# Sixteen gate panels of an encoder layer as four plain panels and six seven-product pairs, and a convolution that adds nine of its taps by transfers

## The chip, the cores and the metric

The kernel runs on one core of a Trainium2 chip. Times are device microseconds (us) of one execution of the whole program; a kernel's time is the median of its runs. The engines are called as in the profile: PE multiplies matrices, DVE is the vector engine, ACT the scalar engine, POOL the GpSimd engine, SP only issues transfers. Each engine works through its own queue in order. POOL's queue holds transfers too: one that waits for a semaphore holds back everything behind it.

## The reference

Two encoder layers on 528 positions (16 meta tokens and 512 tokens) by 2048 channels. What the change touches lies in the first:

```python
u = rmsnorm(h, norm_g)
proj = jnp.einsum("bld,de->ble", u, w_in)
z_a, xs, Bm, Cm, dt_f, dt_b, z_b, glu_v, glu_g = split_cols(proj, IN_E_SIZES)
y_a = ssd_mixer(xs, Bm, Cm, dt_f, dt_b, z_a, ...)
# conformer_conv: GLU, a 31-tap depthwise convolution, LayerNorm over channels, SiLU
y_b = conformer_conv(glu_v, glu_g, dw_w, dw_b, ln_g, ln_b) * jax.nn.silu(z_b)
return h + jnp.einsum("ble,ed->bld", jnp.concatenate([y_a, y_b], axis=-1), w_out)
```

The second layer (neighbourhood attention) and the final norm are not touched.

## The kernel before, in words

Activations lie with channels on the partitions: a tile is 128 channels by 528 positions, 16 tiles for 2048 channels. A **panel** is 128 output columns of a weight. `proj` multiplies one panel: both factors are split in a high and a low part (`wh`, `wl` of the weight, `rh`, `rl` of the input), three products are kept, and with 16 tiles of input and two halves of 264 positions that is 96 matmuls of 128x264. `fetch` makes the halves of a weight: a transfer to `raw`, a copy on ACT to `wh` (L256), a subtraction on DVE to `wl` (L259).

A **seven-product pair** (`sproj`) makes two panels at once by a scheme with seven block products in place of eight: 168 matmuls for 192. It needs sums of weight blocks (`block_ops`; a transfer with accumulation on POOL's queue, L169, and additions on DVE, L176), seven blocks per pair, sums of input tiles (`combos`, L803, eight of them, each with four half-tile additions and two splits on DVE; the tiles come in by transfers to a ring of slots `srt`), and merging additions (`merge`). The last of the sums is written over the split input itself (`fourth`, tiles `sr4`). A `phase` first makes four plain panels while the sums are formed, then six pairs.

The program runs in this order.

- **Scan and GLU stage**: the panels of the state-space scan, group by group, and between them the GLU panels. Each finished GLU tile `u` (buffer `up`) goes to `conv31` (L438): two taps on ACT as the start of `a0` and `a1`, 29 taps as multiply-and-add on DVE (L447), alternately into `a0` and `a1`, their sum (L449), a store to `cv_d`, and an addition to `accl`. A queue `bgc` holds the convolutions; `step` lets some taps run after every panel. The POOL multiplication `sg` (L656) stands before the multiplication into `u` (L659).
- **Second gate** (L743 to L758): 16 plain panels `z_b`, each evacuated by DVE (L746) with SiLU on ACT, all kept in SBUF. Remaining taps run there, then the LayerNorm `ln`: a column sum of `accl` on PE gives the mean, 16 tiles are loaded from `cv_d` into 16 buffers, the mean is subtracted (L722), squares are summed, the reciprocal root is made, and each tile is scaled (L737), gets SiLU, is multiplied by its gate (L739) and stored to `yb_d`.
- **Phases a, b, c** (L920): the output projection over `yz_d` (a), over `yb_d` (b), and the next layer's projections (c), each four panels and six pairs. The next phase's input is split during the last pair of the one before.

The order on each engine is not the order of the text: a scheduler orders the recorded instructions by its own estimate of when each is ready.

Of the kernel before, what the change touches and what calls it, by code (L numbers as in the profile page):

```python
# [12 lines left out]
F32 = mybir.dt.float32  # L13
# [4 lines left out]
P = 128  # L18
# [45 lines left out]
EARLY = 4  # L64
SRB, SRC = 5, 3
# [17 lines left out]
def hybrid_encoder(ctx: ExitStack, tc: tile.TileContext, hT, win, wdt, wout, oin, oout, par, con,  # L83
# [34 lines left out]
    yz_d = dr.tile([KT, P, L], F32, name="yz_d")  # L118
    cv_d = dr.tile([KT, P, L], F32, name="cv_d")
# [9 lines left out]
    gcut = [0, 1, 2, 3, 4, 6, 7, 8, 10]  # L129
# [6 lines left out]
    panels += [win[48 + m] for m in range(KT)]  # L136
    vqk = [oin[b + p] for p in range(KT) for b in (32, 0, 16)]
    for seq in ([wout[0, (m + 2 * NORM) % KT] for m in range(KT)], [wout[1, m] for m in range(KT)], vqk):
        panels += seq[:2 * NORM]
        panels += [(seq[2 * j], seq[2 * j + 1], 3 if j == NORM else int(2 * j + 2 == len(seq))) for j in range(NORM, len(seq) // 2)]  # L140
# [229 lines left out]

    gstack = ctx.enter_context(ExitStack())
    gp = gstack.enter_context(tc.tile_pool(name="gp", bufs=1))

    with ExitStack() as c0:
# [63 lines left out]
        def conv31(i, u):  # L438
            wv = lambda j: pr("dw", KC * i + j, KC * i + j + 1)
            a0 = gp.tile([P, L], F32, name="a0", tag="a0", bufs=1)  # L440
            a1 = gp.tile([P, L], F32, name="a1", tag="a1", bufs=1)
            nc.scalar.activation(a0, u[:, 15:15 + L], AF.Identity, bias=pr("db", i, i + 1), scale=wv(15))  # L442
            nc.scalar.activation(a1, u[:, 14:14 + L], AF.Identity, scale=wv(14))
            rest = [j for j in range(KC) if j not in (14, 15)]
            for q, j in enumerate(rest):
                a = (a0, a1)[q % 2]
                nc.vector.scalar_tensor_tensor(a, u[:, j:j + L], wv(j), a, op0=ALU.mult, op1=ALU.add)  # L447
                yield 620
            nc.vector.tensor_tensor(a0, a0, a1, op=ALU.add)  # L449
            nc.gpsimd.dma_start(cv_d[i], a0)  # L450
            yield 620
            if i == 0:
                nc.scalar.activation(accl, a0, AF.Copy)
            else:
                nc.vector.tensor_tensor(accl, accl, a0, op=ALU.add)
            yield 620
# [16 lines left out]
        sg0 = gp.tile([P, L], F32, name="sg", tag="sig", bufs=1)  # L473
# [173 lines left out]
        def step():  # L647
            pump(bgs, SB_)
            pump(bgc, CB_)

        def glu_tile(i):
            ps = proj(us, ls)
            sg = gp.tile([P, L], F32, name="sg", tag="sig", bufs=1)
# [4 lines left out]
            ps = proj(us, ls)  # L658
            u = gp.tile([P, L + KC - 1], F32, name="up", tag="up", bufs=3)  # L659
# [31 lines left out]
    srn = [0]  # L691

    def slot(name="srt"):
        i = srn[0] % (SRB + SRC) if len(sr) > 1 else 0
        srn[0] += 1
        return sr[i >= SRB].tile([P, L], F32, name=name, tag="srt")
# [6 lines left out]

    ready = {}

    with ExitStack() as c1:
        psb = c1.enter_context(pool(name="psc", bufs=1, space=bass.MemoryType.PSUM))
        zb = c1.enter_context(pool(name="zbp", bufs=14))
        big = c1.enter_context(pool(name="big", bufs=16))
        rp = c1.enter_context(pool(name="rp", bufs=1))  # L710
        mu = accl
        zbs = []
        xc = []
        acq = rp.tile([P, L], F32, name="acq")

        def ln():
            nc.vector.tensor_scalar_mul(h2(mu), colsum([accl], psb, "cs"), 1.0 / D)
            yield 600
            for i in range(KT):
                t = big.tile([P, L], F32, name="xc", tag="xc")  # L720
                nc.gpsimd.dma_start(t, cv_d[i])
                nc.vector.tensor_tensor(t, t, mu, op=ALU.subtract)  # L722
                xc.append(t)
                sq = tp.tile([P, L], F32, name="sq", tag="st", bufs=2)
                if i == 0:
                    nc.scalar.activation(acq, t, AF.Square)
                else:
                    nc.scalar.activation(sq, t, AF.Square)
                    nc.vector.tensor_tensor(acq, acq, sq, op=ALU.add)
                yield 1250  # L730
            rsl = mu
            rstd_row(acq, L, CH, psb, "cs", rsl)
            yield 1500
            for i in range(KT):
                while len(zbs) <= i:
                    yield 1000
                nc.vector.scalar_tensor_tensor(xc[i], xc[i], pr("lg", i, i + 1), rsl, op0=ALU.mult, op1=ALU.mult)  # L737
                nc.scalar.activation(xc[i], xc[i], AF.Silu, bias=pr("lb", i, i + 1))
                nc.vector.tensor_tensor(xc[i], xc[i], zbs[i], op=ALU.mult)  # L739
                nc.gpsimd.dma_start(yb_d[i], xc[i])  # L740
                yield 1250

        for m in range(KT):  # L743
            ps = proj(us, ls)
            t = zb.tile([P, L], F32, name="zb", tag="zb")
            nc.vector.tensor_tensor(h2(t), ps, rs0h, op=ALU.mult)  # L746
            nc.scalar.activation(t, t, AF.Silu)
            zbs.append(t)
            if bgc:
                pump(bgc, 7000)  # L750
# [848 lines left out]
```

## Time and profile before

| | us |
|---|---|
| median of 3 runs (lowest, highest) | 2637.94 (2636.39, 2638.48) |
| the profiled execution | 2635.41 |
| its span | 2633.6 |
| PE busy | 2599.0 (99%) |
| DVE busy | 2050.0 (78%) |
| ACT busy | 1417.3 (54%) |
| POOL busy | 363.2 (14%) |
| first and last evacuation of the second gate (L746) | 1109.2, 1289.3 |
| first and last scaling in phase a (L961) | 1307.0, 1462.2 |
| last sum of a convolution's two halves (L449) | 1183.1 |

All rows of the trace are of this one execution, 2.5 us under the median. Its span leaves 1.8 us outside. A duration in a row is that of one instruction alone; when DVE's instructions follow each other closely, the next one starts before the last has ended, so a queue's pace is read from the starts in a timeline and not from the durations.

### The profile page before, as it was taken

Reading aid. Unit: us, or ns where it says so; the run is one execution under the profiler, and the core shown is the slowest. Engines: PE = TensorE matmul, PEld = TensorE weight load, DVE = VectorE, ACT = ScalarE, POOL = GpSimd, SP = SyncE. Lnnn points to the kernel's source line nnn. Section 1 sums busy time; section 2 is a strip of 40 time slices with the busy share of each in tenths; the row PEclk is TensorE's granted clock in tenths of the full one; section 3 lists DMA queues with packets and bytes.
Section 4 is the critical chain, followed back from the end, with each engine's and each line's share of the span. In section 5 each row is a group of like instructions: output and inputs, shape, how many; then the busy total and the mean of one; then the engine's idle time right before and its main releaser. Section 6 shows DMA issues by size and latency. Waiting matters only on the chain.

```text
span 2633.6 us, 52655 instructions
## 1 busy us (share of the span) xinstructions
PE 2599.0 (99%) x21236; PEld 2485.8 (94%) x21236; DVE 2050.0 (78%) x3046; ACT 1417.3 (54%) x2636; POOL 363.2 (14%) x586
## 2 busy tenths in 40 slices
PE   8999999999999999999999999999999999999997
PEld 8999999999999999999999999999999987777797
DVE  6985967887686969997688888877777776666886
ACT  5366585666658566325554556633334355656543
POOL 0000000000000001100220312200000043443133
PEclk9999999999999999999999999999999999999999
DMA  4222223222222222533875877755555554443755
GB/s 173 98 76 93 81 77 97 81 94 74 92 85 76 88 90 92 177 108 112 266 234 166 296 217 229 239 159 157 157 156 148 151 144 134 135 131 117 232 171 166
DMA packets 147140, 373.40 MB, mean 142 GB/s; under 512 B 32704, under 2 KB 50784, under 8 KB 146896
## 3 DMA queue, kind: packets, MB, share of 16 engines
q1 hardware_dynamic: 121872, 290.09, 34.2%
q0 software_dynamic: 23008, 78.30, 11.2%
q8 instruction: 167, 2.74, 0.4%
q10 hardware_dynamic: 2016, 1.65, 0.2%
q14 instruction: 77, 0.63, 0.1%
HBM read 320.59 MB, written 49.38 MB: 140 GB/s over the span
## 4 chain that ended last, share of the span: by engine, by line
PE 88%; DVE 4%; ACT 4%; issue 2%; DMA 2%; POOL 0%; DVEq 0%; SPq 0%; ACTq 0%; POOLq 0%
PE ps L303 45%; PE pb L280 28%; PE ps L1179 6%; PE py L633 2%; PE po L1165 1%; PE st L573 1%; DVE a L447 1%; DVE wl L259 1%; PE pq L1116 1%; ACT wh L256 1%; ACT T L601 1%; ACT L603 1%; DMA srt<-h_d 1%; ACT sb L1122 1%; PE pa L1140 1%
## 5 line engine op out<-in xcount | busy, mean ns | idle before, releaser
L303 PE MATMUL ps<-rh,wh 128*128 128x264 f32 (+1 forms) x3520 | 730.7, 287 | 9.8 <-ACT rh L320 8.2
L303 PE MATMUL ps<-rh,wl 128*128 128x264 f32 (+1 forms) x3520 | 730.2, 287 | 0.0
L303 PE MATMUL ps<-rl,wh 128*128 128x264 f32 (+1 forms) x3520 | 725.8, 287 | 1.3 <-DVE rl L321 1.2
L256 ACT ACTIVATE wh<-raw 128x1024 fp32r<-128x1024 f32 (+1 forms) x349 | 369.1, 1057 | 528.9 <-PE ps L303 271.7
L259 DVE TENSOR_TENSOR wl<-raw,wh 128x1024 fp32r<-128x1024 f32 (+1 forms) x349 | 440.5, 1262 | 161.9 <-ACT wh L256 157.1
L303 PEld LDWEIGHTS ps<-rh,wh 128*128 128x128 f32 (+1 forms) x3520 | 549.3, 188 | 16.1 <-ACT rh L320 9.0
L303 PEld LDWEIGHTS ps<-rl,wh 128*128 128x128 f32 (+1 forms) x3520 | 546.5, 188 | 4.8 <-DVE rl L321 2.2
L303 PEld LDWEIGHTS ps<-rh,wl 128*128 128x128 f32 (+1 forms) x3520 | 548.9, 188 | 2.1
L280 PE MATMUL pb<-rh,wh 128*128 128x264 f32 (+1 forms) x1280 | 364.1, 285 | 1.0 <-ACT wh L256 1.0
L280 PE MATMUL pb<-rh,wl 128*128 128x264 f32 (+1 forms) x1280 | 363.1, 284 | 0.0
L280 PE MATMUL pb<-rl,wh 128*128 128x264 f32 (+1 forms) x1280 | 363.0, 284 | 0.0
L447 DVE SCALAR_TENSOR_TENSOR a<-up,prm,a 128x528 f32<-128x528 f32 x464 | 343.2, 770 | 2.3 <-ACT a L442 0.9
L280 PEld LDWEIGHTS pb<-rh,wh 128*128 128x128 f32 x1280 | 241.2, 188 | 1.8 <-ACT wh L256 1.2
L280 PEld LDWEIGHTS pb<-rl,wh 128*128 128x128 f32 x1280 | 241.1, 188 | 0.0
L280 PEld LDWEIGHTS pb<-rh,wl 128*128 128x128 f32 x1280 | 240.4, 188 | 0.1
L280 PE MATMUL pb<-ta,wh 128*128 128x264 f32 (+1 forms) x1280 | 236.1, 283 | 0.4 <-ACT wh L256 0.4
L280 PEld LDWEIGHTS pb<-ta,wh 128*128 128x128 f32 x1280 | 198.2, 188 | 0.7 <-ACT wh L256 0.6
L256 ACT ACTIVATE wh<-wy 128x1024 fp32r<-128x1024 f32 x109 | 115.5, 1059 | 138.2 <-PE pb L280 98.5
L280 PE MATMUL pb<-ta,wl 128*128 128x264 f32 (+1 forms) x640 | 182.0, 285 | 2.6 <-DVE wl L259 2.4
L259 DVE TENSOR_TENSOR wl<-wy,wh 128x1024 fp32r<-128x1024 f32 x109 | 138.1, 1268 | 58.7 <-ACT wh L256 58.5
L256 ACT ACTIVATE wh<-wb 128x1024 fp32r<-128x1024 f32 x80 | 84.7, 1059 | 99.6 <-PE pb L280 75.3
L280 PEld LDWEIGHTS pb<-ta,wl 128*128 128x128 f32 x640 | 120.3, 188 | 3.4 <-DVE wl L259 3.4
(389 smaller groups left out, 4119.1 us busy)
## 6 DMA issues: line engine op xcount, KB each, us to landing
raw<-win SPq DMA_DIRECT2D x192, 512.0 KB, 3.7
raw<-oin SPq DMA_DIRECT2D x84, 512.0 KB, 4.5
raw<-wout SPq DMA_DIRECT2D x40, 512.0 KB, 5.5
wb<-oin SPq DMA_DIRECT2D x22, 512.0 KB, 3.9
wy<-oin SPq DMA_DIRECT2D x22, 512.0 KB, 3.4
wy<-oin POOLq DMA_DIRECT2D x22, 512.0 KB, 7.3
raw<-oout SPq DMA_DIRECT2D x20, 512.0 KB, 4.9
srt<-h_d POOLq DMA_DIRECT2D x38, 264.0 KB, 5.3
```

The source lines that it names most:

```text
L256: nc.scalar.activation(wh, raw, AF.Copy)
L259: nc.vector.tensor_tensor(wl, raw, wh.bitcast(F32), op=ALU.subtract)
L280: nc.tensor.matmul(o, w[:, k, :], u[:, lo:lo + n], start=(new and k == 0 and j == 0), stop=(k == KH - 1 and j == 2), skip_group_check=not new)
L303: nc.tensor.matmul(ps[:M, n, :N], w[:, k, :], u[:, lo + n * N:lo + (n + 1) * N], start=(kk == 0 and j == 0), stop=(kk == KT - 1 and j == 2))
L447: nc.vector.scalar_tensor_tensor(a, u[:, j:j + L], wv(j), a, op0=ALU.mult, op1=ALU.add)
L573: nc.tensor.matmul(st[:, :nd * 256], xb[:, c, 256:], xd[:, d0:d1].rearrange("p r x -> p (r x)"), start=True, stop=True)
L601: nc.scalar.activation(T[:, d, c * CH:(c + 1) * CH], pf[:CH, c // 3, (c % 3) * CH:(c % 3 + 1) * CH], AF.Relu, bias=fcol[:, c, d, hd:hd + 1 ...
L603: nc.scalar.activation(h2(cq[:, d]), pf[:, :, :HL], AF.Exp)
L633: nc.tensor.matmul(py[j * HD:(j + 1) * HD, c // 3, (c % 3) * CH:(c % 3 + 1) * CH], a, b, start=(q == 0), stop=(q == nt - 1))
L1116: nc.tensor.matmul(pqs[a, w][:, :n], x[hs, w * P:(w + 1) * P], y[hs, st:st + n], start=(j == 0), stop=(j == 2))
L1122: nc.scalar.activation(sv, sv, AF.Exp, bias=mx, scale=-1.0, accum_out=self.sm[a][:, w:w + 1])
L1179: nc.tensor.matmul(ps, w[:, k, :], u[:, lo:lo + S], start=(kk == 0 and j == 0), stop=(kk == KT - 1 and j == 2))
```

## The change

- The second gate becomes a `phase`: four plain panels, then six seven-product pairs. Each gate tile is stored by SP to a new buffer in memory, `zb_d`, in place of being kept.
- Of each convolution's 29 taps on DVE, nine (four for tiles 12 to 15) become a product on ACT (`pt`) and a transfer on POOL's queue that adds it to `a1` in SBUF. All other taps go into `a0`. `more` issues them, two with every `step`.
- `ln` works from memory: each tile is loaded from `cv_d`, centred, stored back; after the reciprocal root it is loaded again, with its gate from `zb_d`, finished, and stored to `yb_d`. All these transfers are on POOL's queue, through the ring of slots. `ln` runs in small pieces (`side`) in the gate and in phase a.
- The tiles `a0`, `a1`, `sg` share three buffers; pair results use the three `up` buffers; the slots are five until the gate's fourth panel, then eight. GLU tiles come earlier (`gcut`): 13 in the groups and 3 behind, for 10 and 6. Phase a's input tiles come on POOL's queue and no longer on SP's.

In the changed kernel a matmul of `proj` is L306, of a pair L283; a tap is L475, the sum of `a0` and `a1` L479, the addition to `accl` L485; a weight's low half is L262, the addition of weight blocks L179, the combination of input tiles L798 to L801, their splits L785 and L788; the evacuation of a gate panel is L979.

**DVE between two gate panels.** Before, from the evacuation of the third gate panel on (tap, low half, tap; `a_12958` and `a_12959` are `a0` and `a1` of one tile):

```order
L746 TENSOR_TENSOR zb<-ps,rs_84 128x528
L447 SCALAR_TENSOR_TENSOR a_12958<-up,prm,a_12958 128x528
L259 TENSOR_TENSOR wl<-raw,wh 128x1024
L447 SCALAR_TENSOR_TENSOR a_12959<-up,prm,a_12959 128x528
L447 SCALAR_TENSOR_TENSOR a_12958<-up,prm,a_12958 128x528
L447 SCALAR_TENSOR_TENSOR a_12959<-up,prm,a_12959 128x528
```

Fifteen instructions stand from this evacuation up to the next. In the changed kernel, from the evacuation of the third gate panel on (`a_12835` and `a_13273` are the `a0` of tiles 14 and 15):

```order
L979 TENSOR_TENSOR cx<-ps,rs_85 128x528
L475 SCALAR_TENSOR_TENSOR a_13273<-up,prm,a_13273 128x528
L262 TENSOR_TENSOR wl<-raw,wh 128x1024
L475 SCALAR_TENSOR_TENSOR a_12835<-up,prm,a_12835 128x528
L685 TENSOR_TENSOR accy<-accy,zt 128x528
L475 SCALAR_TENSOR_TENSOR a_13273<-up,prm,a_13273 128x528
L479 TENSOR_TENSOR a_12835<-a_12835,a_12836 128x528
L475 SCALAR_TENSOR_TENSOR a_13273<-up,prm,a_13273 128x528
L485 TENSOR_TENSOR accl<-accl,a_12835 128x528
L475 SCALAR_TENSOR_TENSOR a_13273<-up,prm,a_13273 128x528 x4
L262 TENSOR_TENSOR wl<-wb,wh 128x1024
L798 TENSOR_TENSOR srt<-srt 128x264
```

From here to the last addition to `accl` stand 48 instructions: 11 taps, 10 more of 128x528, 5 of 128x1024 (three low halves and two additions of weight blocks) and 22 of half a tile. The end of that stretch:

```order
L785 SCALAR_TENSOR_TENSOR tb_13315<-srt,tb_13314 128x264
L479 TENSOR_TENSOR a_13273<-a_13273,a_13274 128x528
L485 TENSOR_TENSOR accl<-accl,a_13273 128x528
L262 TENSOR_TENSOR wl<-raw,wh 128x1024
L799 TENSOR_TENSOR srt<-srt 128x264
L798 TENSOR_TENSOR srt<-srt 128x264
L179 TENSOR_TENSOR raw<-raw 128x1024
L949 TENSOR_SCALAR accl<-cs 128x528
```

Before, this addition to `accl` stood among plain gate panels; now it stands between the third panel and the fourth.

**PE at the same place.** After the third gate panel come three blocks of the first pair, 24 matmuls each, then the column sum of `accl`, then the fourth panel (with what a row waits for):

```order
L283 MATMUL pb_13766<-rl_208,wh_13629 128x264
L283 MATMUL pb_13766<-rh_207,wl_13630 128x264
L331 MATMUL cs_13511<-accl_87,cst_72 128x264 [waits DVE_49]
L331 MATMUL cs_13511<-accl_87,cst_72 128x264
L306 MATMUL ps_13527<-rh_147,wh_13262 128x264 [waits PE_49]
L306 MATMUL ps_13527<-rh_147,wh_13262 128x264
```

The column sum waits for DVE, and the fourth panel stands behind it.

**POOL at the same place.** The store of tile 14, then the four additions to `a1` of tile 15 (L492), with accumulating weight transfers and slot loads between them:

```order
L480 DMA cv_d_78<-a0_12835 128x528 [waits DVE_49]
L492 DMA a1_13274<-pt_13320 128x528 [waits DMASW7_49,Activation_49]
L172 DMA wy_13049<-win 128x1024 [waits DMAHW2_49,DMASW0_49]
L172 DMA wy_13635<-win 128x1024 [waits DMAHW4_49,DMASW1_49]
L745 DMA srt_13642<-hT 128x528 [waits DMASW6_49,DMASW2_49,DVE_49]
L492 DMA a1_13274<-pt_13323 128x528 [waits DMASW7_49,DMASW3_49]
L745 DMA srt_13284<-hT 128x528 [waits DMASW4_49,DVE_49]
L745 DMA srt_13301<-hT 128x528 [waits DMASW5_49,DVE_49]
L745 DMA srt_13303<-hT 128x528 [waits DMAHW5_49]
L492 DMA a1_13274<-pt_13441 128x528 [waits DMASW3_49]
L745 DMA srt_13473<-hT 128x528 [waits DMAHW6_49,DMASW0_49,DVE_49]
L492 DMA a1_13274<-pt_13445 128x528 [waits DMASW7_49,DMASW1_49,Activation_49]
```

The first of them stands behind a store that waits for DVE, and each later one waits for a transfer before it.

The diff, cut to its core:

```diff
+NPROD = (9, 4)
+LATEC = 12
+SIDE = 1300
...
-    gcut = [0, 1, 2, 3, 4, 6, 7, 8, 10]
+    gcut = [0, 1, 3, 5, 7, 8, 10, 11, 13]
...
-    panels += [win[48 + m] for m in range(KT)]
...
-    for seq in ([wout[0, (m + 2 * NORM) % KT] for m in range(KT)], [wout[1, m] for m in range(KT)], vqk):
+    for seq in ([win[48 + m] for m in range(KT)], [wout[0, (m + 2 * NORM) % KT] for m in range(KT)], [wout[1, m] for m in range(KT)], vqk):
...
+    def side(budget, n=2):
+        if bgc:
+            for _ in range(n):
+                bgc[0].more()
+            pump(bgc, budget)
+        else:
+            pump(bgs, budget)
+
+    def drain(limit):
+        while len(bgc) > limit:
+            bgc[0].more()
+            pump(bgc, 620)
...
-            rest = [j for j in range(KC) if j not in (14, 15)]
-            for q, j in enumerate(rest):
-                a = (a0, a1)[q % 2]
-                nc.vector.scalar_tensor_tensor(a, u[:, j:j + L], wv(j), a, op0=ALU.mult, op1=ALU.add)
+                rest = [j for j in range(KC) if j not in (14, 15)]
+                n = NPROD[i >= LATEC]
+                self.prods = self.products(a1, rest[:n])
+                for j in rest[n:]:
+                    nc.vector.scalar_tensor_tensor(a0, u[:, j:j + L], wv(j), a0, op0=ALU.mult, op1=ALU.add)
+                    yield 620
+                while self.prods:
+                    yield 1e9
+                nc.vector.tensor_tensor(a0, a0, a1, op=ALU.add)
+                nc.gpsimd.dma_start(cv_d[i], a0)
...
+            def products(self, a1, js):
+                for j in js:
+                    p = tp.tile([P, L], F32, name="pt", tag="st", bufs=2)
+                    nc.scalar.activation(p, self.u[:, j:j + L], AF.Identity, scale=self.wv(j))
+                    nc.gpsimd.dma_start(a1, p, accum_op=ALU.add)
+                    yield
...
         def step():
             pump(bgs, SB_)
-            pump(bgc, CB_)
+            side(CB_)
...
             ps = proj(us, ls)
+            drain(2)
             u = gp.tile([P, L + KC - 1], F32, name="up", tag="up", bufs=3)
...
+                side(2 * SIDE)
             ta, tb = next(gen)
...
+                    def hook(i):
+                        next(gen, None)
+                        if j > NORM and i in (0, 2, 4):
+                            side(SIDE)
...
+        def ln():
+            ps = colsum([accl], psp[0], "ps")
+            nc.vector.tensor_scalar_mul(h2(mu), ps, 1.0 / D)
+            yield 600
+            for i in range(KT):
+                t = stream(cv_d[i])
+                nc.vector.tensor_tensor(t, t, mu, op=ALU.subtract)
+                nc.gpsimd.dma_start(cv_d[i], t)
...
+                yield 1300
+            rstd_row(rsl, L, CH, psp[0], "ps", rsl)
+            yield 1500
+            for i in range(KT):
+                while nzb[0] <= i:
+                    yield 1e9
+                t, z = stream(cv_d[i]), stream(zb_d[i])
...
+                nc.gpsimd.dma_start(yb_d[i], t)
+                yield 1300
+
+        def done_z(m, t, ps):
+            if t is None:
+                drain(max(0, 2 - m))
+                more[0] = m > 2
+                t = xy("cx")
+                nc.vector.tensor_tensor(h2(t), ps, rs0h, op=ALU.mult)
+            else:
+                nc.vector.tensor_tensor(t, t, rs0, op=ALU.mult)
+            nc.scalar.activation(t, t, AF.Silu)
+            nc.sync.dma_start(zb_d[m], t)
+            nzb[0] = m + 1
+
+        bgs.append(ln())
+        phase(lambda k: hT[k], "eg", done_z, after=following(lambda k: yz_d[k], "sg"), given=[(us, ls)], drain=False)
```

147 lines of the change are left out of this document (60 added, 87 removed).

## The prediction

> **What bounds the kernel now.** I read the page's first table, then the waits of PE, then the stretch that the change rewrites, by stages.
>
> ```profile
> span 2633.6 us, 52655 instructions
> PE 2599.0 (99%) x21236; PEld 2485.8 (94%) x21236; DVE 2050.0 (78%) x3046; ACT 1417.3 (54%) x2636; POOL 363.2 (14%) x586
> ```
>
> PE is the bound of the whole. All waits of PE from 1040 to 1480 us, so from the last GLU panels to the end of phase a, are one row:
>
> ```profile
> PE ps L303 <- ACT rh L317: 1.4, 1, 1.4
> ```
>
> The busy times of the engines in three stretches: a full one in the scan stage, the second gate, phase a (after the times: PE, PEld, DVE, ACT, POOL, clock, DMA share, GB/s):
>
> ```profile
> 153.00:203.00 50.00, 50.00 (x398) 48.36 (x397) 48.96 (x71) 31.16 (x74) 0.72 (x3) 1.00 0.26 88
> 1109.20:1289.90 180.70, 180.70 (x1493) 180.57 (x1492) 146.83 (x200) 79.85 (x104) 13.74 (x26) 1.00 0.40 136
> 1289.90:1479.10 189.20, 187.78 (x1541) 187.56 (x1541) 150.73 (x215) 92.47 (x130) 38.14 (x66) 1.00 0.76 237
> ```
>
> PE has no gap, at full clock. DVE is busy 81% of the gate and 80% of phase a: whatever the change brings DVE there must fit in about 34 and 38 us, and at the right place. In the first stretch DVE is full (48.96 of 50.00) and PE still waits for nothing, so a full DVE alone is no loss; a DVE that stands behind PE's need is.
>
> **What the change takes from PE.** The pace of a matmul, from the starts in PE's timeline (the last column but one counts instructions):
>
> ```profile
> 1199.93 0.41 PE L303 MATMUL ps<-rh,wl 128*128 128x264 f32 x2
> 1200.17 0.41 PE L303 MATMUL ps<-rh,wh 128*128 128x264 f32 x2
> 1200.42 0.40 PE L303 MATMUL ps<-rl,wh 128*128 128x264 f32 x2
> 1200.66 0.40 PE L303 MATMUL ps<-rh,wl 128*128 128x264 f32 x2
> ```
>
> Three steps of two matmuls take 0.73 us: 0.122 us each. A plain panel of 96 is 11.7 us, a pair of 168 is 20.5. Two rows agree, each with a little beside the panels:
>
> ```profile
> L746 DVE TENSOR_TENSOR zb<-ps,rs x16: 698/707/708, 1109.2 to 1289.3; 128x528 f32<-128x528 f32 x16
> L961 DVE TENSOR_TENSOR cy<-cy,rsa x6: 700/701/704, 1357.9 to 1462.2; 128x528 f32<-128x528 f32 x6
> ```
>
> Fifteen panels in 180.1 us are 12.0 each, five pairs in 104.3 us 20.9 each. Six pairs with 24 matmuls less are 144 × 0.122 = **17.5 us** off PE; nothing else of PE's work goes. Were PE never to wait, that would be the gain.
>
> **What it moves on DVE, and where.** It takes 124 taps from DVE, nearly all of them before the gate, where PE waits for nothing: no gain. Into the first panels of the gate it brings the eight combinations, the additions of weight blocks and the centring, and there stand also 32 taps of tiles 14 and 15. DVE's pace when it has no pause, from starts in its timeline, two places:
>
> ```profile
> 173.46 0.75 DVE L447 SCALAR_TENSOR_TENSOR a<-up,prm,a 128x528 f32<-128x528 f32 x1
> 174.13 0.75 DVE L434 SCALAR_TENSOR_TENSOR cv<-xp,prm,cv 128x528 f32<-128x528 f32 x1
> 174.81 0.76 DVE L447 SCALAR_TENSOR_TENSOR a<-up,prm,a 128x528 f32<-128x528 f32 x1
> ...
> 1300.62 0.42 DVE L813 TENSOR_TENSOR srt<-srt 128x264 f32<-128x264 f32 x1
> 1300.97 0.42 DVE L812 TENSOR_TENSOR srt<-srt 128x264 f32<-128x264 f32 x1
> 1301.31 0.70 DVE L801 TENSOR_TENSOR ta<-srt,ta 128x528 fp32r<-128x528 f32 x1
> 1301.93 0.42 DVE L798 SCALAR_TENSOR_TENSOR tb<-srt,tb 128x264 fp32r<-128x264 f32 x1
> ...
> 1304.61 1.22 DVE L259 TENSOR_TENSOR wl<-raw,wh 128x1024 fp32r<-128x1024 f32 x1
> 1305.74 0.70 DVE L801 TENSOR_TENSOR ta<-srt,ta 128x528 fp32r<-128x528 f32 x1
> ```
>
> So a tap takes 0.68, half a tile 0.345, another 128x528 0.62, a 128x1024 1.13 us of the queue. From the evacuation of the third gate panel, which must wait for PE, to the last addition to `accl` stand 48 instructions: 11 taps (7.5 us), 10 more of 128x528 (6.2), 5 of 128x1024 (5.7), 22 halves (7.6), **27.0 us**. PE has in this time only three blocks of 24 matmuls, 72 × 0.122 = **8.8 us**, and then the column sum, which waits for that `accl`; the fourth panel is queued behind the column sum. In the queues' own terms, DVE alone makes PE wait 27.0 − 8.8 = **18.2 us**. The two gate panels ahead give no lead: DVE's queue there is about as long as PE's, and an evacuation can't run before its panel.
>
> **What the transfers add there.** The last `accl` needs the four products of tile 15, added one after the other by transfers, the first behind the store of tile 14, which is ready 5.0 us after the evacuation (three taps, three of 128x528, one of 128x1024). With L for one accumulation the sum is 5.0 + 4 L + 1.2 (two additions). No row shows an accumulation from SBUF; the nearest:
>
> ```profile
> wy<-oin SPq DMA_DIRECT2D x22, 512.0 KB, 3.4
> wy<-oin POOLq DMA_DIRECT2D x22, 512.0 KB, 7.3
> wy<-wout POOLq DMA_DIRECT2D x12, 512.0 KB, 7.9
> cv_d<-a POOLq DMA_DIRECT2D x16, 264.0 KB, 2.4
> xc<-cv_d POOLq DMA_DIRECT2D x16, 264.0 KB, 4.9
> ```
>
> The accumulation into `wy` takes 7.3 us where the plain transfer of that size takes 3.4. Bounds for L are 2.4 (the plain store of 264 KB, no charge for adding) and 7.3 (the larger accumulation). I take 2.4 × 7.3 / 3.4 = 5.2, an estimate: the sum is then 27.0, just as long as DVE's own queue. At 2.4 it is 15.8 and DVE decides; at 7.3 it is 35.4, a wait of 26.6. Slot loads that wait for DVE stand between the second addition and the fourth, so I take **20 us** for this wait; bounds 17 (DVE 6% quicker than my paces) and 27.
>
> The Trainium skill has a rule for L, in "DMA: Bandwidth & Descriptors", section "Anatomy of one DMA — SWDGE (gpsimd) path": a transfer issued by GpSimd costs about 2.0 us and its bytes at 436 GB/s. For 264 KB that estimate is 2.6 us, and the store's row (2.4) agrees; for the accumulation of 512 KB it is 3.2, and the row (7.3) does not. By that rule L is 2.6 and the wait stays at DVE's 18.2 us.
>
> **Behind it.** From that `accl` to the second pair's second low half, DVE has 70 more instructions (13 of 128x1024, 24 of 128x528, 33 halves: 14.7 + 14.9 + 11.4 = 41.0 us), PE 292 matmuls, 35.6 us. PE waits another 5.4: **5 us**, bounds 2 and 8. Later DVE's queue between pairs is 16 to 18 us against 20.5, and 26 at the gate's end, where the next phase's input is split: what it loses there it has gained before.
>
> **LayerNorm through memory.** Each centred tile needs its load, and loads stand on POOL behind stores that wait for the subtraction before. A load is 4.9 us (`xc<-cv_d`), and by the paces above the subtractions stand 1 to 9 us apart in DVE's queue in the first two pairs, with loads ahead in the five slots. I take **3 us** of PE waiting, bounds 0 and 10. The second half (16 tiles of 0.68 + 0.62 us, 21 us of DVE) goes to phase a, under whose 188 us of PE work it fits in 38 free; without that room it would cost its 21 us.
>
> **Costed at nothing.** ACT gets 124 products:
>
> ```profile
> L443 ACT ACTIVATE a<-up,prm 128x528 f32<-128x528 f32 x16 | 11.6, 726 | 5.2 <-DVE a L449 5.2
> ```
>
> Each 0.73, so 90 us on an engine that is busy 54%; uncovered it would be those 90. SP's 16 gate stores and POOL's slot loads lie under the panels. In the scan stage POOL adds two products a panel, 2 × 5.2 = 10.4 us of 11.7; a convolution's nine take 47 of the 69 us between GLU tiles (1109 us before the gate, 16 tiles). What is queued behind a waiting addition there is `sg` (L656), for which the GLU tile, and then PE's buffer, wait. PE's lead of one panel, 11.7 us, covers two additions.
>
> **The sum.** −17.5 + 20 + 5 + 3 = +10.5 us. The profiled execution took 2635.4, so 2645.9; it is 2.5 under the median, which gives **2648 us**, slower by 0.4%. Its own range, from the bounds: −17.5 + 17 + 2 + 0 = +1.5 (2639) to −17.5 + 27 + 8 + 10 = +27.5 (2665).
>
> **Rivals.**
>
> *All is hidden*: 2637.9 − 17.5 = 2620 us. For it speaks that PE shows one wait of 1.4 us in 440 us, though DVE was full before too. Against it: 27.0 us on an in-order queue against 8.8. It needs the taps of the last two tiles to be gone before the third panel.
>
> *No change*: the DVE queue is 6% quicker, the wait behind it shrinks to 2, accumulations take 2.4 and loads are in time: +1.5, 2639 us. For it: in the full stretch of 50 us above, my paces sum to 50.4 us although DVE paused for 1 of them.
>
> *POOL's queue becomes the bound of the scan stage*: slower by far. Place: `sg` behind the accumulations.
>
> ```profile
> L656 POOL TENSOR_TENSOR sg<-sg,rs x15: 1316/1322/3947, 137.2 to 1087.1; 128x528 f32<-128x528 f32 x15
> ```
>
> Nine accumulations and one `sg` of 1.3 us fill the 69 us between GLU tiles when L is 7.5: there it starts to decide. At 7.9 (the `wout` row) they are 72.4 us, 3.4 late for each of 12 tiles, 41, less PE's lead of 11.7: 29 us; the seam then costs 5.0 + 31.6 + 1.2 − 8.8 = 29. −17.5 + 29 + 5 + 3 + 29 = +48.5, 2686 us. For it in the profile: POOL's waits for its own accumulations are long already.
>
> ```profile
> POOL wy L169 <- DMA wy<-oin: 359.8, 20, 20.1
> ```
>
> Against it: these cost PE nothing, and an addition here moves half the bytes.
>
> **How the numbers follow.** The forecast has a chance of 0.58, all hidden 0.13, no change 0.17, POOL's queue 0.12. A measurement of this kernel can tell about 0.2% (5.3 us) from no change. Faster is the hidden case and 0.05 of the no-change case: 0.18. Same is 0.12 of the latter and 0.07 at the forecast's lower end: 0.19. Slower is the rest: 0.63. The range is 2624 to 2675: it takes in the forecast's own and reaches part of the way to the hidden case and to POOL's.
>
> **What would show it.** Right: PE waits for DVE or for a transfer once, some 17 to 27 us long, at the column sum behind the third gate panel, with DVE full from the second panel on; a second, shorter one at a low half of the second pair; pairs of 20.5 us after; scan stage and phase b as before. If the column sum's wait ends at a transfer, L was above 5.2; at an addition of DVE that itself had no pause, below. Wrong: PE without a gap there (hidden), or the first gate panel later than 1109 us (POOL's queue), or waits above 10 us in phase a, which I cost at nothing.

## The result and the profile after

The changed kernel takes 2798.25 us (median of 4 runs, 2792.51 to 2801.11), the kernel before in the same comparison 2638.01: 1.0606 times as long, 95% interval 1.0586 to 1.0626. That is 160 us slower. Slower was forecast, by 10; the range ended at 2675.

Three stretches of both kernels show where it went: from 48 us to the first evacuation of a gate panel, from there to the end of phase a, and the rest. The rows give the span's piece, then busy time and instructions of PE, PEld, DVE, ACT and POOL, PE's granted clock, DMA share, GB/s. Before:

```profile
48.00:1109.20 1061.20, 1059.03 (x9115) 1026.95 (x9114) 848.30 (x1157) 637.70 (x1365) 53.36 (x84) 1.00 0.28 92
1109.20:1463.00 353.80, 353.80 (x2914) 353.67 (x2913) 288.01 (x399) 167.50 (x227) 46.49 (x81) 1.00 0.57 181
1463.00:2633.60 1170.60, 1146.15 (x8907) 1066.48 (x8905) 885.04 (x1451) 583.45 (x1001) 260.78 (x402) 1.00 0.59 173
```

After:

```profile
48.00:1194.00 1146.00, 1083.05 (x9062) 1046.68 (x9061) 796.57 (x1060) 714.97 (x1473) 146.55 (x191) 0.97 0.41 109
1194.00:1609.00 415.00, 362.31 (x2817) 355.68 (x2815) 341.42 (x496) 219.69 (x322) 109.02 (x192) 0.93 0.75 233
1609.00:2793.60 1184.60, 1154.13 (x8909) 1072.88 (x8907) 883.57 (x1452) 584.22 (x1001) 257.76 (x404) 0.99 0.57 171
```

A stretch minus PE's busy time is PE's idle time. What PE is busy longer for the same matmuls (in the middle stretch, longer than 17.5 us less than before) is put down to its slower clock; the column of the granted clock falls in the same stretches, to 0.97, 0.93 and 0.99.

| | longer by | more idle | slower clock | saved |
|---|---|---|---|---|
| scan and GLU stage | 84.8 | 60.8 | 24.0 | |
| gate and phase a | 61.2 | 52.7 | 26.0 | −17.5 |
| phase b and later | 14.0 | 6.0 | 8.0 | |
| sum | 160.0 | 119.5 | 58.0 | −17.5 |

**The scan stage.** PE's waits there (total, times, longest, us):

```profile
PE pf L639 <- ACT cq L644: 26.3, 9, 6.6
PE py L674 <- DVE pv L626: 13.7, 4, 4.7
PE py L674 <- ACT cq L644: 7.6, 7, 1.3
PE st L614 <- DVE xd L609: 6.0, 5, 3.1
```

PE waits for the scan's own small operations on ACT and DVE, not for a GLU tile. What holds ACT and POOL (rows of the whole run, nearly all of it in this stage):

```profile
POOL a L492 <- DMA a<-pt: 239.3, 70, 5.4
POOL sg L697 <- ACT sg L696: 175.9, 15, 27.8
ACT pt L491 <- DMA a<-pt: 165.7, 69, 5.3
```

ACT waits 165.7 us for one of the two product buffers, each of which is free only when its accumulation has landed; `sg` waits for ACT, not for accumulations. ACT's timeline (start, duration, what it waited for in brackets):

```profile
211.26 0.73 ACT L491 ACTIVATE pt<-up,prm 128x528 f32<-128x528 f32 x1 [2.83 <-DMA a<-pt]
211.91 1.04 ACT L259 ACTIVATE wh<-raw 128x1024 fp32r<-128x1024 f32 x1
214.88 0.74 ACT L491 ACTIVATE pt<-up,prm 128x528 f32<-128x528 f32 x1 [1.94 <-DMA a<-pt]
219.65 0.74 ACT L491 ACTIVATE pt<-up,prm 128x528 f32<-128x528 f32 x1 [4.03 <-DMA a<-pt]
220.29 1.04 ACT L259 ACTIVATE wh<-raw 128x1024 fp32r<-128x1024 f32 x1
```

The products come in a burst, one every 4 us or so, not two a panel, and a weight's `wh`, `cv`, `cq` stand behind each. One accumulation is short:

```profile
a<-pt POOLq DMA_DIRECT2D x124, 264.0 KB, 3.5
```

**The gate and phase a.** PE's pauses from the third gate panel to the column sum, in the three blocks of the first pair that stand there:

```profile
1219.74 0.39 PE L283 MATMUL pb<-rh,wh 128*128 128x264 f32 x1 [0.91 <-ACT wh L259]
1222.62 0.39 PE L283 MATMUL pb<-rh,wl 128*128 128x264 f32 x1 [2.37 <-DVE wl L262]
1233.25 0.59 PE L283 MATMUL pb<-rh,wh 128*128 128x264 f32 x1 [6.15 <-ACT wh L259]
1234.51 0.59 PE L283 MATMUL pb<-rh,wl 128*128 128x264 f32 x1 [0.45 <-DVE wl L262]
1245.26 0.59 PE L283 MATMUL pb<-rh,wh 128*128 128x264 f32 x1 [6.68 <-ACT wh L259]
```

At the seam stand several pauses of up to 6.7 us rather than one. The column sum waits 4.0 after them, from 1251.3 to 1255.3. Two rows of the other engines say what these waits end at:

```profile
1232.14 1.06 ACT L259 ACTIVATE wh<-wb 128x1024 fp32r<-128x1024 f32 x1 [6.20 <-DMA wb<-win]
1253.79 0.71 DVE L479 TENSOR_TENSOR a<-a,a 128x528 f32<-128x528 f32 x1 [2.65 <-DMA a<-pt]
```

The first is the `wh` of the 6.15 us pause, held by a weight transfer. The second stands right before the last addition to `accl`: DVE waits there for the last accumulation of tile 15. Behind the gate, the longest single pause begins before phase a's first scaling:

```profile
PE cr L352 <- DVE r L347: 10.3, 1, 10.3
```

It is LayerNorm's reciprocal root: the step of DVE it needs stood behind input combinations that waited for their slot loads on POOL's queue.

**The clock.** Windows of 4 us in the scan stage, around pauses of PE (after PE's busy time, its instructions; the clock is the third number from the end):

```profile
212.00:216.00 4.00, 0.29 (x8) 0.29 (x10) 4.00 (x6) 1.68 (x2) 0.98 (x2) 1.00 0.56 101
216.00:220.00 4.00, 4.00 (x61) 3.80 (x57) 2.98 (x5) 0.35 (x1) 0.18 (x1) 0.57 0.67 174
220.00:224.00 4.00, 4.00 (x34) 4.00 (x34) 2.63 (x4) 2.53 (x4) 0.88 (x2) 1.00 0.48 93
...
232.00:236.00 4.00, 0.00 (x0) 0.00 (x0) 1.90 (x2) 3.97 (x10) 1.42 (x2) 0.69 0.58 123
236.00:240.00 4.00, 2.48 (x11) 2.48 (x12) 2.47 (x4) 3.96 (x6) 0.85 (x1) 0.50 0.84 211
240.00:244.00 4.00, 4.00 (x34) 4.00 (x32) 2.79 (x4) 3.97 (x10) 0.85 (x1) 0.96 0.52 84
```

After a pause of about 4 us the clock is near half (0.57 and 0.50), and back to full or nearly so within another 4 (1.00 and 0.96). The Trainium skill says so in "TensorE: Matmul & The Clock Gate", section "Part 1: The HAM clock gate (the 'warmup' mystery)": after an idle window of about 3.4 us the clock falls to half, and a busy window of that length brings it back. The trace agrees, with the four numbers just given.

### The profile page after: what moved, and what is told of

It is laid out like the page before. It is cut to its first block, busy times and chain, and to the rows that moved or that the text cites. A ratio compares the mean times of both kernels' runs of the same rounds, so it can differ in the third digit from the quotient of the medians.

```text
span 2793.6 us, 53114 instructions
## 1 busy us (share of the span) xinstructions
PE 2640.3 (95%) x21092; PEld 2514.8 (90%) x21092; DVE 2050.3 (73%) x3047; ACT 1547.7 (55%) x2839; POOL 515.9 (18%) x804
## 4 chain that ended last, share of the span: by engine, by line
PE 38%; DMA 7%; DVE 5%; issue 4%; ACT 3%; POOL 1%; DVEq 0%; SPq 0%; POOLq 0%; ACTq 0%
PE pb L283 26%; PE ps L1218 5%; PE ps L306 3%; DVE wl L262 2%; DMA t_d<-srt 1%; ACT wh L259 1%; PE po L1204 1%; ACT sb L1161 1%; DMA a<-pt 1%; DMA srt<-yz_d 1%; DMA srt<-cv_d 1%; DMA srt<-yb_d 1%; PE pq L1155 1%; PE pa L1179 1%; DMA yb_d<-srt 1%
## 5 line engine op out<-in xcount | busy, mean ns | idle before, releaser
L306 PE MATMUL ps<-rh,wh 128*128 128x264 f32 (+1 forms) x3136 | 660.0, 290 | 11.8 <-ACT rh L323 8.5
L306 PE MATMUL ps<-rl,wh 128*128 128x264 f32 (+1 forms) x3136 | 661.3, 290 | 0.7 <-DVE rl L324 0.6
L306 PE MATMUL ps<-rh,wl 128*128 128x264 f32 (+1 forms) x3136 | 655.9, 289 | 0.0
L262 DVE TENSOR_TENSOR wl<-raw,wh 128x1024 fp32r<-128x1024 f32 (+1 forms) x340 | 432.5, 1272 | 215.5 <-ACT wh L259 210.7
L306 PEld LDWEIGHTS ps<-rh,wh 128*128 128x128 f32 (+1 forms) x3136 | 497.0, 191 | 16.2 <-ACT rh L323 9.3
L306 PEld LDWEIGHTS ps<-rl,wh 128*128 128x128 f32 (+1 forms) x3136 | 496.8, 191 | 5.6 <-DVE rl L324 1.8
L306 PEld LDWEIGHTS ps<-rh,wl 128*128 128x128 f32 (+1 forms) x3136 | 496.3, 191 | 2.7 <-DVE wl L262 0.2
L283 PE MATMUL pb<-rh,wh 128*128 128x264 f32 (+1 forms) x1472 | 422.4, 287 | 19.5 <-ACT wh L259 14.8
L283 PE MATMUL pb<-rh,wl 128*128 128x264 f32 (+1 forms) x1472 | 420.2, 286 | 3.3 <-DVE wl L262 3.3
L283 PE MATMUL pb<-rl,wh 128*128 128x264 f32 (+1 forms) x1472 | 420.3, 286 | 0.0
L283 PEld LDWEIGHTS pb<-rh,wh 128*128 128x128 f32 x1472 | 280.0, 190 | 21.9 <-ACT wh L259 16.4
L283 PEld LDWEIGHTS pb<-rh,wl 128*128 128x128 f32 x1472 | 279.3, 190 | 4.1 <-DVE wl L262 4.1
L283 PE MATMUL pb<-ta,wh 128*128 128x264 f32 (+1 forms) x1472 | 277.8, 287 | 4.4 <-ACT u L862 2.7
L283 PEld LDWEIGHTS pb<-rl,wh 128*128 128x128 f32 x1472 | 280.1, 190 | 0.0
L475 DVE SCALAR_TENSOR_TENSOR a<-up,prm,a 128x528 f32<-128x528 f32 x340 | 257.7, 763 | 2.9 <-ACT a L469 0.2
L283 PEld LDWEIGHTS pb<-ta,wh 128*128 128x128 f32 x1472 | 232.5, 192 | 5.7 <-ACT u L862 2.9
L283 PE MATMUL pb<-ta,wl 128*128 128x264 f32 (+1 forms) x736 | 212.7, 290 | 15.4 <-DVE wl L262 15.2
L492 POOL DMA_DIRECT2D a<-pt x124 | 106.7, 861 | 556.2 <-DMA a<-pt 239.3
L262 DVE TENSOR_TENSOR wl<-wy,wh 128x1024 fp32r<-128x1024 f32 x124 | 155.6, 1255 | 63.5 <-ACT wh L259 63.2
L491 ACT ACTIVATE pt<-up,prm 128x528 f32<-128x528 f32 x124 | 90.3, 743 | 166.3 <-DMA a<-pt 165.7
```

The lines of the kernel that those rows point to most:

```text
L262: nc.vector.tensor_tensor(wl, raw, wh.bitcast(F32), op=ALU.subtract)
L283: nc.tensor.matmul(o, w[:, k, :], u[:, lo:lo + n], start=(new and k == 0 and j == 0), stop=(k == KH - 1 and j == 2), skip_group_check=not new)
L306: nc.tensor.matmul(ps[:M, n, :N], w[:, k, :], u[:, lo + n * N:lo + (n + 1) * N], start=(kk == 0 and j == 0), stop=(kk == KT - 1 and j == 2))
L475: nc.vector.scalar_tensor_tensor(a0, u[:, j:j + L], wv(j), a0, op0=ALU.mult, op1=ALU.add)
L491: nc.scalar.activation(p, self.u[:, j:j + L], AF.Identity, scale=self.wv(j))
L492: nc.gpsimd.dma_start(a1, p, accum_op=ALU.add)
```

## The experiments

Each kernel but the last was run once, beside a run of the kernel before on the same chip (2634.3 to 2634.5 us). The kernel before lay between 2631.9 and 2638.7 us over all its runs, so a difference of a few microseconds between two single runs is not read. "Gate" is from the first to the last evacuation or scaling of a gate panel, "phase a" likewise; before they are 180.1 and 155.2 us.

### Is it the products?

No products, all else as changed:

```diff
-NPROD = (9, 4)
+NPROD = (0, 0)
```

> The changed kernel with all 29 taps of every convolution on DVE again, in one chain on a0; the gate's pairs and the LayerNorm through memory stay. In the changed kernel the first gate panel is evacuated at 1194.0 us, 84.8 later than before; from there to phase a's last scaling it takes 414.4 us, before 353.0. Theory A (products held in ACT's queue until an accumulation frees one of two buffers) and theory B (POOL's multiplication sg queued behind accumulations) both say: the first gate panel comes at 1108 to 1115 us. Theory C (the scan stage loses by the other order of GLU tiles, the shared buffers or the single chain): it stays above 1150. For the gate: if the seam is DVE's queue, as forecast, 120 taps more on DVE leave it as long or longer, 414 us or more to phase a's end, total about 2710 to 2730; if the wait there comes from the accumulations, it is under 380, total under 2690.

The products alone, on the kernel before:

```diff
         def step():
             pump(bgs, SB_)
-            pump(bgc, CB_)
+            side(CB_)
...
             ps = proj(us, ls)
+            drain(2)
...
-                pump(bgc, 7000)
+                side(7000)
```

(and `conv31`, `side` and `drain` of the changed kernel.)

> The kernel before with the products and their accumulating transfers alone (nine, four for tiles 12 to 15, with the rule that lets no more than two convolutions wait); gate as sixteen plain panels, LayerNorm in SBUF, GLU tiles in their old places. Theories A and B: the scan stage loses most of the 85 us here too, first gate panel at 1160 to 1200, total 2690 to 2730. Theory C: below 1125, total below 2655.

Measured: without products 2705.5 us, first gate panel at 1106.2 (both slightly below what was expected, 2710 to 2730 and 1108 to 1115); with the products alone 2720.4, first gate panel at 1196.0, gate 177.8. So the scan stage's 85 us belong to the products, all of them, and neither to the order of the GLU tiles nor to the shared buffers. The rows of the kernel with the products alone show that nothing else is lost in it:

```profile
48.00:1196.00 1148.00, 1085.55 (x9128) 1050.01 (x9127) 789.83 (x1047) 713.82 (x1485) 145.75 (x200) 0.97 0.42 112
1196.00:1373.80 177.80, 177.80 (x1469) 177.67 (x1468) 139.15 (x187) 81.32 (x107) 20.36 (x33) 1.00 0.48 150
```

Without products the gate and phase a still take 414.6 us, as long as with them (414.4): taking the accumulations away does not shorten them. Since DVE has more taps there without products, this alone does not show that the accumulations cost nothing there.

### Which part of the products?

```diff
-                    nc.scalar.activation(p, self.u[:, j:j + L], AF.Identity, scale=self.wv(j))
+                    nc.gpsimd.tensor_scalar_mul(p, self.u[:, j:j + L], self.wv(j))
```

> The changed kernel with the products made by POOL in place of ACT; their transfers stand behind them on the same queue. Theory A: ACT never waits for a product's buffer, so PE's waits for cq and wh in the scan stage go: first gate panel at 1110 to 1130, total 2725 to 2740. Theory B: POOL gets 124 multiplications more, sg comes later still: first gate panel at 1194 or later, total 2798 or more.

```diff
-NPROD = (9, 4)
+NPROD = (4, 4)
```

> The changed kernel with four products for every tile, 64 in place of 124. Theory A: with two buffers and about 4 us each the waits shrink faster than the count: first gate panel at 1120 to 1145, a third or less of the 85 us. Theory C: 1180 or later. The gate and phase a take the 414 us of the changed kernel, 10 more or less.

Four products: 2722.2, first gate panel at 1123.4. ACT's waits for a buffer fall from 165.7 to 40.7 us, the stage's loss (against no products) from 87.8 to 17.2: more than in proportion to the 64 of 124, as expected. The gate and phase a take 411.1 us, as expected too.

Products on POOL: 2832.0, first gate panel at 1234.2, and theory A had said 1110 to 1130. It fell as it stood. Theory B expected the time, but its cause, `sg`, is not what PE waits for: ACT makes no products there, and now DVE waits, in its own queue, for the last accumulation of a convolution:

```profile
DVE a L479 <- DMA a<-pt: 137.2, 12, 16.1
```

PE's three longest waits in the scan stage are for DVE then (46.9, 28.6 and 22.4 us in total). So it seems not to matter which engine makes the products, but that an engine with other work waits for a serial chain of transfers. A product takes POOL about 2.1 us, where ACT takes 0.73, so this run changes the pace of the chain too. I sharpened the theory, and took away the chain; the destination and the addition change with it, and DVE's sum of `a0` and `a1` no longer waits for a transfer:

```diff
-                    nc.gpsimd.dma_start(a1, p, accum_op=ALU.add)
+                    nc.gpsimd.dma_start(pj_d[9 * self.i + js.index(j)], p)
```

> The changed kernel, but each of the 124 products goes by a plain transfer to a place of its own in memory and is not added: nine (four) taps of each convolution are left out. The 90 us of products on ACT, their two buffers, the transfers and POOL's issues stay; what goes is that each transfer waits for the one before. Theory A, sharpened (the serial additions hold the two buffers, and through them ACT's queue): first gate panel at 1106 to 1125, total 2705 to 2735. Rival (ACT's 90 us of work, or the traffic): 1150 or later, total above 2750.

2702.2 us, first gate panel at 1113.4. With the same 124 products on ACT, the same two buffers and as many transfers, but none that waits for the one before, 80.6 of the 84.8 us are gone (the total is 3 us below what was expected). One transfer is hardly shorter, 3.1 us against 3.5, yet ACT's waits for a buffer fall from 165.7 to 55.1: so it is the chain, much more than the length of one transfer:

```profile
48.00:1113.40 1065.40, 1055.68 (x9058) 1025.32 (x9057) 792.71 (x1061) 716.48 (x1476) 107.29 (x195) 1.00 0.35 118
```

The gate and phase a still take 407.5 us, with DVE's taps as in the changed kernel: about 7 us of their 61 more than before, at most, come from the accumulations. No run gave the products more than two buffers or spread their bursts, so whether either would have saved the stage is open.

### What holds the gate?

All on the kernel without products. All GLU tiles inside the groups:

```diff
-    gcut = [0, 1, 3, 5, 7, 8, 10, 11, 13]
+    gcut = [0, 2, 4, 6, 8, 10, 12, 14, 16]
```

> No products, and all 16 GLU tiles inside the groups, two in each, so that the last convolutions end before the gate. The forecast's seam (DVE's queue with the last taps ahead of accl, a wait of 16.3 us at the column sum without products): that wait falls under 5 us and the gate, from first to last evacuation, from 213.9 us to 185 to 200; total 2675 to 2695. If instead the combinations and weight sums alone overload DVE there: gate above 205, total 2700 or more.

LayerNorm only from the gate's second pair on:

```diff
-                side(2 * SIDE)
+                if bgc or not given:
+                    side(2 * SIDE)
```

> No products, and LayerNorm through memory starts only in the second pair of the gate; the fourth panel is no longer behind the column sum, and the centring leaves the seam. Seam theory: the wait at the column sum goes, the other waits for low halves stay, gate 190 to 205 us; but LayerNorm's later half falls on phase a, which then takes as much more as the gate gains if transfers on POOL's queue set its end: total 2690 to 2710. If LayerNorm's transfers were not the limit of phase a: total 2680 to 2690.

Both:

> Both edits of the two runs before on the kernel without products. If the seam's 82 us of DVE work are the cause, the gate comes near PE's own time (four panels and six pairs after the first evacuation, about 160 us): 165 to 185 us from first to last evacuation; total 2670 to 2690, the rest lost in phase a. If not: within 5 us of the better of the two.

In the two with the GLU tiles inside, the second GLU tile's panels and the first group's are used in another order than they were loaded, so what they compute is not the reference's result; the work is the same. They took 2721.7 and 2714.4 us, slower than without the edit, and gates of 260.4 and 240.7 where 185 to 200 and 165 to 185 were expected. By the numbers that is the other branch of the first expectation (gate above 205, total 2700 or more). But the edit also moved the last group of the scan behind the GLU tiles and so into the gate's first panels; from the first gate panel on PE waits 13.0 and 11.8 us for its `cq`. They tell nothing clean of the seam.

LayerNorm late: 2693.4. The wait at the column sum (16.3 us without products) went, the four plain panels ran without a pause (1105.8 to 1143.2), and then the first pair took as long as all had before: its last scaling came 102.5 us after the first evacuation, 103.2 with LayerNorm in the seam. The gate took 208.0 us where 190 to 205 were expected, and phase a 184.3, no more than without the edit (184.2), though the expectation let the gate's gain come back there. DVE in the first 27 us of that pair is full, and PE waits:

```profile
1143.00:1170.00 27.00, 16.75 (x94) 14.99 (x93) 27.00 (x47) 14.28 (x22) 4.88 (x9) 0.75 0.55 171
```

So most of the wait had moved. The next run takes work from DVE there, 28 of 29 taps of tiles 13 to 15:

```diff
-                for j in rest[n:]:
+                for j in rest[n:] if i < 13 else rest[-1:]:
```

> The kernel with LayerNorm late and no products, with 28 of the 29 taps of tiles 13 to 15 left out on DVE (so the output is not the reference's): up to 84 x 0.68 = 57 us less on DVE around the first gate panels. With the taps the first pair's last scaling came 102.5 us after the first gate evacuation (1105.8 to 1208.3), PE's own work for it is 57. If the first pair is late because DVE's queue is full there (theory D, the forecast's seam, larger than forecast), it comes 60 to 75 us after. If it is late for the combinations' transfers or for POOL (theory E), 90 or more. Total by D about 2655 to 2670, by E 2685 or more.

2670.5, and the first pair's end 79.8 us after the first evacuation: between the two expectations, nearer to theory D. The taps are 23 of the 46 us that the first pair comes late. The rest was not taken apart: the combinations, weight sums and centring keep DVE busy 50.2 of the 55 us from 1140 to 1195 even then, which fits theory D, but PE's waits there end more often on ACT (a `wh`, 4.5 us in total) than on DVE (a `wl`, 2.4), and what those `wh` wait for was not followed.

> The kernel without products, with eight plain panels and four pairs in the gate (NORM of the gate 4): the combinations are spread over eight panels, the last taps drained over five. PE saves 4 x 24 x 0.122 = 11.7 us in place of 17.5. Theory D: counted as in the forecast, DVE is 11 us behind PE at the eighth panel in place of 19 at the fourth, so PE waits 25 to 35 us less than in the kernel without products: total 2665 to 2680. If the pairs as such are slow there: 2700 or more.

```diff
+NORMZ = 4
...
-            for m in range(2 * NORM):
+            for m in range(2 * norm):
...
-                drain(max(0, 2 - m))
-                more[0] = m > 2
+                drain(max(0, 2 - m // 2))
+                more[0] = m > 5
```

Eight plain panels: 2680.4, 25 us less than with four although 5.8 fewer are saved on PE. That is theory D's direction but less than its size: PE is idle 19.8 us less, where 25 to 35 were expected. Gate 197.0. What is left in the gate is one wait, in the place that the forecast had named:

```profile
PE cs L333 <- DVE accl L487: 19.9, 1, 19.9
```

### What holds phase a?

The second half of LayerNorm left out, from the reciprocal root on:

```diff
-                nc.gpsimd.dma_start(cv_d[i], t)
+                nc.gpsimd.dma_start(yb_d[i], t)
...
-            rstd_row(rsl, L, CH, psp[0], "ps", rsl)
...
```

(and the whole loop behind it.)

> The kernel without products, with the second half of LayerNorm left out (no reciprocal root, no scale, SiLU and gate product; the centred tiles go to yb_d), so phase a has only its own work. With it phase a takes 184.2 us from first to last scaling (1336.6 to 1520.8), before 155.2. Theory F (the 16 tiles from memory and the second reciprocal root hold DVE and PE in phase a): 153 to 162, and the gap of 16.5 us between the gate's last and phase a's first scaling falls to about 12; total about 2670 to 2680. If phase a is slow for its own input from POOL's queue: 175 or more, total above 2690.

2669.3, phase a 155.2 us from first to last scaling (1334.7 to 1489.9), just as before the change. Theory F holds: the 29 us that phase a is longer with it are LayerNorm's second half. The gap ahead of phase a stayed at 15.9 us, where about 12 was expected; but PE works through all of it now, where it had been idle 9.2 of 16.5 us. Two rows, phase a with and without that half:

```profile
1336.60:1521.50 184.90, 172.79 (x1339) 169.49 (x1340) 149.98 (x212) 90.21 (x126) 52.25 (x94) 0.96 0.77 246
```

```profile
1334.70:1490.60 155.90, 154.36 (x1259) 153.51 (x1259) 128.63 (x179) 77.28 (x107) 27.88 (x48) 1.00 0.70 211
```

DVE has 35 us free in the first, and PE waits all the same. 16.1 of the 35 us are DVE's waits for LayerNorm's own loads (`cv_d` 9.4, `zb_d` 6.7). PE's longest wait is again for the reciprocal root, just ahead of phase a's first scaling:

```profile
PE cr L352 <- DVE r L347: 10.1, 1, 10.1
```

From the gate's last scaling to phase a's end the half costs 29.6 us: 19.8 of PE's idle time, and 9.8 in which PE is busy longer, at a clock of 0.79 in the gap and 0.96 behind it where it was 1.00.

### All findings in one

No products, eight plain panels, and:

```diff
-                side(2 * SIDE)
+                if bgc or not given or m >= 6:
+                    side(2 * SIDE)
...
-                t, z = stream(cv_d[i]), stream(zb_d[i])
+                for n in range(i + len(ahead2), min(i + 2, nzb[0])):
+                    ahead2.append((stream(cv_d[n]), stream(zb_d[n])))
+                t, z = ahead2.popleft()
```

> All findings in one working kernel: no products, eight plain panels and four pairs in the gate, LayerNorm begins only behind the seventh panel, and in its second half the loads of a tile and its gate are issued one tile ahead. Of the kernel with eight plain panels (2680.4) the wait of 19.9 us at the column sum and about 9 us at a lower clock should go, and some of the 21 us that phase a takes longer than before: 2640 to 2655. Against the kernel before it would still be the same or slower by up to 0.8%. If the wait only moves to the first pair: 2670 or more.

2675.3 us (4 runs, 2673.5 to 2678.2), 1.0146 times the kernel before, 1.0129 to 1.0163. The wait at the column sum is gone and the gate takes 183.4 us, 13.6 less than with eight plain panels alone; but that is no less than sixteen plain panels take (180.1), and phase a takes 6.2 more (181.8) and what follows 5.1 more. The time lies above the 2640 to 2655 expected, where the expectation had put the case that the wait only moves; what is left of it in the gate is one wait of 6.3 us for a `wh`. No version tried beats the kernel before.

### The clock over all runs

Idle time is the span less PE's busy time, 34.6 us before; the clock's part is PE's busy time less 2599.0, with 17.5 (11.7 for eight plain panels, nothing for the products alone) added. The first 48 us count here too, so the changed kernel's numbers differ by 0.8 from the table further up; without LayerNorm's second half 24 matmuls are missing too:

| | more idle, us | clock, us |
|---|---|---|
| LayerNorm late, last taps out | 33.0 | 19.6 |
| all findings in one | 34.7 | 19.6 |
| LayerNorm's second half out | 38.5 | 12.8 |
| eight plain panels | 41.1 | 15.5 |
| LayerNorm late | 47.2 | 28.2 |
| products without the chain | 58.1 | 26.3 |
| products alone | 58.3 | 26.7 |
| no products | 60.9 | 26.5 |
| GLU tiles inside, LayerNorm late | 63.9 | 32.6 |
| four products | 70.1 | 34.2 |
| GLU tiles inside | 73.2 | 30.5 |
| changed kernel | 118.7 | 58.8 |
| products on POOL | 158.7 | 55.4 |

With each microsecond that PE waits more go another 0.3 to 0.6 at a lower clock. That the pauses cause the slow clock is read from the order of the windows above and from this table; no run paused PE on purpose.

## Why the prediction was wrong, step by step

**Right: what PE saves, and the place and the sum of the seam; partly by luck.** No run gainsays the 17.5 us, and the pace of a pair after the first is near PE's own (five pairs in 103.2 us, 20.6 each, against 20.5). PE's idle time from the first gate evacuation to the first pair's end (1194.0 to 1301.4) was 21.2 + 4.3 = 25.5 us, where the forecast had 20 + 5. DVE's 48 instructions took 27.6 us of its queue, against 27.0. That DVE's load there costs PE time is borne out by the run without the last taps and by the one with eight plain panels, both without products.

The waits themselves were others. The forecast put one wait of 17 to 27 us at the column sum; there were several of up to 6.7. The two longest are for a `wh` on ACT: one waited 6.2 us for a weight transfer, the other stood in ACT's queue until a combination on DVE was done. DVE paused 7.5 us in those 48 instructions (twice for a `wh`, once for the last accumulation), where the forecast had let it run through. Of the 4.3 us, 2.7 are a wait for ACT in the first pair; at the low half of the second pair, where the forecast had its 5, stand 2.6. And a column sum that waits for a transfer was to mean an L above 5.2: it did wait for one, with L at 3.5, because tile 15's four accumulations were issued 5 to 10 us apart (1226.2, 1236.2, 1243.7, 1248.9), with weight transfers and slot loads between them. So 25.5 against 25 is in part luck.

**Wrong, the largest: "Costed at nothing", the scan stage.** 85 us: 60.8 of PE's idle time and 24.0 put down to the clock. This is the step that failed, in three places. It took two products a panel, where the scheduler had put them in bursts. It set the nine accumulations against the time between GLU tiles, as if only their sum counted. And it named `sg` as what is queued behind them, and PE's buffer behind that; what was queued behind was ACT's own work for the scan, since a product waits on ACT (165.7 us in total) for a buffer that a transfer frees. Without products the loss is gone, and without the chain 80.6 of the 84.8 us. L itself was overestimated: 5.2 taken, 3.5 measured (3.2 to 8.6). The rival on POOL's queue had the right stage and the wrong queue: with L at 3.5 its point of decision, 7.5, was never near. The prediction's own signs of being wrong came: the first gate panel at 1194.0 us instead of 1109, and a wait above 10 us at phase a.

**Wrong: "LayerNorm through memory", its second half.** 21 us of DVE were held against 38 free and called hidden. The 29 us of phase a are LayerNorm's second half, as the run without it shows. The free time was there and of little use: in the kernel without products DVE waited 16.1 us of it for the loads of the items, and weights' low halves stand behind the items in its queue (PE waits 5.7 us for them). And the forecast had no term for the reciprocal root, which stands in PE's own queue and held it 10.3 us (10.1 without products).

**Missing: the clock.** 58 us in the changed kernel. The forecast priced a wait at its own length; here another half went with it. On the seam alone that is an estimate of 12 us more: PE was busy 55.8 and 26.1 us there at a granted clock of 0.84 and 0.89. That the waits cause it is argued, not shown, as said above.

**The sum.** −17.5 + 25.5 for the seam + 3.7 in the later pairs stands against −17.5 + 25 + 3. What was forecast as nothing came to 60.8 us of idle time in the scan stage, 23.5 from the gate's last scaling to phase a's end, 6.0 later, and 58.0 of clock: 160.0 in all. Slower was forecast and came, but not for the reason that made the forecast slower: the seam and the later pairs, less what PE saves, are 12 of the 160 us.

## What to carry to other kernels

An offload to transfers is not priced by their sum but by who waits for them: ask of each buffer that a transfer frees which engine's queue stands still until then, and what is behind. An engine's free share in a stage does not show that work which must first be loaded will fit in it, as long as the queue is in order. And where PE sets the time, a pause can cost more than its length; here 0.3 to 0.6 us at a lower clock went with each microsecond.

## What the runs showed of the hardware that I had not expected

An accumulating transfer of 264 KB from SBUF to SBUF landed 3.5 us after its issue (median of 124; 3.2 to 8.6), well under the 7.1 us of an accumulation of 512 KB from memory (the row before had 7.3) and a little above the 2.4 us of a plain store of its size; a chain of them ran at one in 4.1 us (nine issues from 207.6 to 240.7). PE's clock was near half (0.50 and 0.57) in the 4 us after a pause of about 4 us, and over all runs the lower clock came to 0.3 to 0.6 of PE's extra idle time.
